# A sixth buffer for the ring of loads in a decoder layer on one core

## The chip, the core and the metric

The kernel runs on one core of a Trainium2 chip. The metric is the time on the device in microseconds (us); less is better. Five engines work side by side, each through its own queue in order: PE (matmul; PEld is its weight load), DVE and ACT (elementwise work), POOL and SP, which issue transfers here. They wait for each other by semaphores. An instruction that waits holds up all that stand behind it on its engine.

## What is computed

One layer of a decoder for 256 tokens of 2048 features, in float32. Cut to what matters here:

```python
mod = silu(c) @ w_ada + b_ada                  # 2048 x 12288: shift, scale, gate, twice
u = x * (1 + scale1) + shift1
proj = u @ w_in                                # 2048 x 9216: GLU input | q | k | v | gate logits
hc = a_lin * sigmoid(a_gate)                   # branch A
hc = silu(layer_norm(causal_depthwise_conv(hc, 31 taps)))
y_conv = hc @ w_conv_out + b_conv_out
y_attn = attention(rope(q), rope(k), v) @ w_attn_out      # branch B: 8 heads, causal
y = (sigmoid(g_A) * y_conv + sigmoid(g_B) * y_attn) @ w_out
x = layer_norm(alpha * x + (1 + gate1) * y)
u = x * (1 + scale2) + shift2
a, val = split(u @ w_up)                       # 2048 x 11264
y = (silu(causal_depthwise_conv(a, 3 taps)) * val) @ w_down
x = layer_norm(alpha * x + (1 + gate2) * y)
```

## The kernel before

All weights are read once from HBM. They come in chunks of 128 rows by 1024 columns (512 KB), 483 of them, called w0, w1, ... here in the order in which they are used. `chunk` (L380) loads a chunk into a `raw` buffer of the pool `st`, casts it on ACT into a high part `wh` (L393), and forms the low part `wl` on DVE by subtracting (L394). `group` (L419) lets PE multiply with it three times (`feat`, L401: L405 high by high, L406 high by the low part of the activations, L407 low by high). The rings hold five `raw` buffers and three each of `wh` and `wl`: the cast of w66 can only start when PE is done with w63.

The matrix w_ada goes past PE: `ada` (L168) loads it in tiles of 512 KB into the same ring of `raw` buffers (the first piece of its columns apart) and sums their rows, weighted by silu(c), on DVE (L207; the first row block on ACT, L205). When a piece of columns is summed over all rows, PE transposes it (L223, eight transposes into two PSUM tiles `pa`), DVE reduces it (L225, two), adds the bias (L234 for the shift, L236 for the scale), and `make_u` (L245) forms four tiles of `u` on ACT (L254), their high parts `uh` (L242), and on DVE their low parts `ul` (L243). A tile of `u` is 128 rows of u, transposed; PE needs tile k for every chunk of w_in that holds rows 128k and up.

The chunks of w_in are taken in an order that lets PE start before all of `u` is there (L655 to L659): w0 to w35 use tiles 0 to 3, w36 to w43 tiles 4 to 7, w44 to w59 tiles 4 to 11, and w60 to w67 are one group with tiles 8 to 15. So w64 is the first that uses tile 12. Chunks w68 to w143 are the rest of w_in, w144 to w159 are w_attn_out, w160 to w175 w_conv_out; then follow w_out, w_up and w_down.

Beside w_in, in the background, run the depthwise conv (L514: products on ACT at L533, sums on DVE at L535 and L531), its layer norm (L538: mean L544, squares L552, variance and square root L557 and L558, reciprocal L560, scaling L566, silu L568, split into `chi` and `clo` at L242 and L243), and the attention of eight heads (L596). In a head the scores `s0` (128 queries by 128 keys) and `s1` (the other 128 queries by 256 keys) get a mask added on DVE (L607 and L608); the left half of the mask for `s1` is zero. Exponentials (L615) follow on ACT. The gates' sigmoids (L490) fall in the same time, and ACT loads a table when it changes between the two. w160, the first chunk of w_conv_out, needs `chi`; the PSUM banks that it writes are freed by four multiplications on DVE (L706).

What stands where in each engine's queue isn't written by hand except at a few places: the framework makes a timeline of its own from the program, its dependencies and its buffers, and orders each engine's instructions by it. So the number of buffers in a ring is one of the things that the order comes from.

Small constants lie in their own tiles: `rows` (L82, six blocks of 128 columns for vectors that PE turns into columns), `rows2` (L113, a seventh), `mask` (L110, 256 columns), `junk` (L218, where L229 writes a copy that nobody reads, since it wants only the row sums), and `bst` (L915, statistics of the last layer norm).

Of the kernel before, what the change touches and what calls it, by code (L numbers as in the profile page):

```python
# [8 lines left out]
F32 = mybir.dt.float32  # L9
F32R = mybir.dt.float32r  # L10
AF = mybir.ActivationFunctionType
OP = mybir.AluOpType
# [21 lines left out]
def layer_kernel(ctx: ExitStack, tc: tile.TileContext, x, c, w_ada, b_ada, w_in, conv_dw_w, conv_dw_b,  # L34
                 conv_ln_g, conv_ln_b, w_conv_out, b_conv_out, w_attn_out, w_out, ln1_g, ln1_b,
                 w_up, ffn_dw_w, ffn_dw_b, w_down, ln2_g, ln2_b, k_ident, k_mask, k_rope, out):
    nc = tc.nc
    x = x[0]
    w_ada, b_ada, w_in, w_conv_out, w_attn_out, w_out, w_up, w_down = (
        t[0] for t in (w_ada, b_ada, w_in, w_conv_out, w_attn_out, w_out, w_up, w_down))  # L40
# [3 lines left out]
    cst = ctx.enter_context(tc.tile_pool(name="cst", bufs=1))  # L44
    big = ctx.enter_context(tc.tile_pool(name="big", bufs=1))
    st = ctx.enter_context(tc.tile_pool(name="st", bufs=5))
    wk = ctx.enter_context(tc.tile_pool(name="wk", bufs=2))
# [5 lines left out]
    def slot(i, shape, dt, name):  # L53
        return big.tile(shape, dt, tag=f"h{i}", name=name)
# [24 lines left out]

# [1 line left out]
    ident = cst.tile([128, 128], F32, name="ident")  # L81
    rows = slot(13, [128, 6, 128], F32, "rows")  # L82
    nc.scalar.dma_start(rows[0:16, 0], c.rearrange("o (r p) -> (o r) p", p=128))
# [19 lines left out]
    ccol, p = columns("ccol", 0, 16)  # L103
# [5 lines left out]
    nc.gpsimd.memset(ones, 1.0)  # L109
    mask = cst.tile([128, 256], F32, name="mask")  # L110
    ropec = cst.tile([128, 256], F32, name="ropec")
    ropes = cst.tile([128, 256], F32, name="ropes")
    rows2 = wk.tile([44, 128], F32, name="rows2", bufs=1)  # L113

    def load_vectors():
        prev = [i for i in traced() if i.engine == mybir.EngineType.SP][-1]

        def put(dst, src):
            nc.gpsimd.dma_start(dst, src)

        r0 = 0
        for ap, n in ((conv_dw_b, 8), (conv_ln_g, 8), (conv_ln_b, 8), (b_conv_out, 16), (ln1_g, 16), (ln1_b, 16),
                      (ffn_dw_b, 44)):
            put(rows[r0:r0 + n, 2], vec(ap))
            r0 += n
        cwr = conv_dw_w.rearrange("k (r p) -> (k r) p", p=128)
        fwr = ffn_dw_w.rearrange("k (r p) -> (k r) p", p=128)
        put(rows[:, 3], cwr[:128])
        put(rows[:120, 4], cwr[128:])
        put(rows[:88, 5], fwr[:88])  # L130
        put(rows2, fwr[88:])
        put(mask, k_mask)
        put(ropec, k_rope[0])
        put(ropes, k_rope[1])

# [1 line left out]
    xT = wide(0, F32, "xT")  # L137
# [19 lines left out]

# [1 line left out]
    mod = cst.tile([128, 96], F32, name="mod")  # L159
# [55 lines left out]
    def to_columns(acc, cols, n, quick=False):  # L215
        w = n * len(cols)
        red = wk.tile([128, 8], F32, tag="red", name="red")
        junk = wk.tile([128, 128], F32, tag="junk", name="junk", bufs=1)  # L218
        for b in range(w // 512):
            p = pst("pa")  # L220
            for i in range(4):
                j = b * 4 + i
                nc.tensor.transpose(p[:, i * 128:(i + 1) * 128], acc[:, j * 128:(j + 1) * 128], ident)  # L223
            if quick:
                nc.vector.tensor_reduce(red[:, b * 4:b * 4 + 4], p.rearrange("p (a b) -> p a b", a=4), AX.X, OP.add)  # L225
            else:
                for i in range(4):
                    j = b * 4 + i
                    nc.scalar.activation(junk, p[:, i * 128:(i + 1) * 128], AF.Copy, accum_out=red[:, j:j + 1])  # L229
        m = n // 128  # L230
# [147 lines left out]

# [1 line left out]
    def chunk(src, width, two=False):  # L380
# [61 lines left out]

# [1 line left out]
    lin = slot(6, [128, 8, 256], F32, "lin")  # L444
# [63 lines left out]

# [1 line left out]
    cacc, chi = [None], []  # L510
# [61 lines left out]

# [1 line left out]
    rps = []  # L574
# [21 lines left out]
    def attention():  # L596
# [4 lines left out]
        def head(h):  # L601
# [4 lines left out]
            p = pp[:, h % 2]  # L606
            nc.vector.tensor_tensor(p[:, 0:128], s0, mask[:, 128:256], OP.add)  # L607
            nc.vector.tensor_tensor(p[:, 128:384], s1, mask, OP.add)  # L608
            mx = wk.tile([128, 6], F32, tag="mx", name="mx")
# [40 lines left out]

# [1 line left out]
    ra0 = 1.0  # L652
# [19 lines left out]
    for i, (g, k0, k1, ra, rb) in enumerate(items):  # L672
# [6 lines left out]
        if i == 12:  # L679
# [11 lines left out]
            p = pst("fw1_ps")  # L691
            nc.tensor.transpose(p[:, :44], rows2, ident[:44, :44])
            fw1 = cst.tile([128, 44], F32, name="fw1")
# [85 lines left out]

# [1 line left out]
    def norm(k, n, center):  # L781
# [38 lines left out]

# [1 line left out]
    NP = 7  # L822
# [49 lines left out]

# [1 line left out]
    lrows = [slot(i, [128, D], F32, n) for i, n in ((14, "l2g"), (15, "l2b"))]  # L874
# [39 lines left out]
    nst = [0, 0]  # L914
    bst = [cst.tile([128, 4 if C2 == 1536 else 5, nc.vector.BN_STATS_DIM], F32, name=f"bst{t}") for t in range(2)]  # L915
    for g, (c0, c1) in enumerate(((0, 1024), (1024, C2), (C2, 2048))):
# [65 lines left out]
```

## Time and profile before

| | us |
|---|---|
| runs | 1475.29, 1480.73, 1479.78 |
| median | 1479.78 |
| span of the profiled execution, first to last instruction | 1477.4 |
| PE busy in it | 1417.7 |
| DVE busy | 1108.8 |
| ACT busy | 796.9 |

The span of the profiled execution lies among the times of the runs, 2.4 us below their median. PE counts as busy from a matmul's start to its end, and matmuls overlap, so short pauses don't show in the busy time. The number behind x in a stretch is the count of matmuls that started in it, and PEclk is the granted clock as a share of 2.4 GHz.

### The profile page before, as it was taken

Reading aid. Unit: us, or ns where it says so; the run is one execution under the profiler, and the core shown is the slowest. Engines: PE = TensorE matmul, PEld = TensorE weight load, DVE = VectorE, ACT = ScalarE, POOL = GpSimd, SP = SyncE. Lnnn points to the kernel's source line nnn. Section 1 sums busy time; section 2 is a strip of 40 time slices with the busy share of each in tenths; the row PEclk is TensorE's granted clock in tenths of the full one; section 3 lists DMA queues with packets and bytes.
Section 4 is the critical chain, followed back from the end, with each engine's and each line's share of the span. In section 5 each row is a group of like instructions: output and inputs, shape, how many; then the busy total and the mean of one; then the engine's idle time right before and its main releaser. Section 6 shows DMA issues by size and latency. Waiting matters only on the chain.

```text
span 1477.4 us, 26835 instructions
## 1 busy us (share of the span) xinstructions
PE 1417.7 (96%) x10691; PEld 1364.2 (92%) x10691; DVE 1108.8 (75%) x1398; ACT 796.9 (54%) x1250; POOL 27.7 (2%) x57
## 2 busy tenths in 40 slices
PE   4899999999999989998999999999999999999996
PEld 4889999989999989997999999999999998888886
DVE  6788888998989879896877767988765545446456
ACT  3546436669987655345545576555444444343342
POOL 2000000210000000000000000000000000000000
PEclk9999999999999999999999999999999999999998
DMA  9999899886567657987799977778776676655662
GB/s 310 328 302 334 299 339 310 256 280 209 175 194 222 210 173 254 310 297 226 242 307 315 323 248 218 240 246 254 238 217 183 180 224 215 193 172 173 189 202 100
DMA packets 154990, 358.53 MB, mean 243 GB/s; under 512 B 12172, under 2 KB 26466, under 8 KB 154608
## 3 DMA queue, kind: packets, MB, share of 16 engines
q1 hardware_dynamic: 152704, 352.37, 74.0%
q0 software_dynamic: 1872, 4.33, 0.9%
q8 instruction: 83, 1.36, 0.4%
q14 instruction: 43, 0.35, 0.1%
q10 hardware_dynamic: 288, 0.12, 0.0%
HBM read 353.10 MB, written 2.10 MB: 240 GB/s over the span
## 4 chain that ended last, share of the span: by engine, by line
PE 75%; DMA 13%; DVE 8%; issue 2%; ACT 2%; SPq 0%; DVEq 0%; ACTq 0%
DMA araw<-in_w_ada_dram 9%; PE acc0a L405 5%; PE acc0a L407 5%; PE acc0a L406 5%; PE acc1a L405 5%; PE acc1a L407 5%; PE acc1a L406 5%; PE acc2a L406 3%; PE acc2a L407 3%; PE acc2a L405 3%; PE acc3a L405 3%; PE acc3a L406 3%; PE acc3a L407 3%; DVE wl L394 3%; DVE acc L207 2%
## 5 line engine op out<-in xcount | busy, mean ns | idle before, releaser
L393 ACT CAST wh<-wraw 128x1024 fp32r<-128x1024 f32 (+1 forms) x483 | 496.7, 1030 | 559.5 <-PE acc3a L416 132.7
L394 DVE TENSOR_TENSOR wl<-wraw,wh 128x1024 fp32r<-128x1024 f32 (+1 forms) x483 | 577.1, 1198 | 252.1 <-ACT wh L393 248.1
L207 DVE SCALAR_TENSOR_TENSOR acc<-araw,ccol,acc 128x1024 f32<-128x1024 f32 (+1 forms) x182 | 225.4, 1238 | 84.3 <-DMA araw<-in_w_ada_dram 82.6
L405 PE MATMUL acc0a<-u2h,wh 128*128 128x256 f32 x352 | 99.3, 282 | 4.8 <-ACT u2h L325 4.8
L407 PE MATMUL acc0a<-u2h,wl 128*128 128x256 f32 x352 | 100.3, 285 | 3.1 <-DVE wl L394 3.1
L405 PE MATMUL acc1a<-u2h,wh 128*128 128x256 f32 x352 | 99.4, 283 | 0.0
L406 PE MATMUL acc0a<-u2l,wh 128*128 128x256 f32 x352 | 99.4, 282 | 0.0
L406 PE MATMUL acc1a<-u2l,wh 128*128 128x256 f32 x352 | 99.2, 282 | 0.0
L407 PE MATMUL acc1a<-u2h,wl 128*128 128x256 f32 x352 | 99.2, 282 | 0.0
L533 ACT ACTIVATE pr<-hc,cw 128x256 f32<-128x256 f32 x200 | 88.8, 500 | 11.7 <-DVE cacc L535 11.3
L405 PE MATMUL acc0a<-uh,wh 128*128 128x256 f32 x256 | 74.9, 292 | 7.1 <-ACT uh L242 7.1
L407 PE MATMUL acc0a<-uh,wl 128*128 128x256 f32 x256 | 74.5, 291 | 3.2 <-DVE wl L394 3.2
L406 PE MATMUL acc0a<-ul,wh 128*128 128x256 f32 x256 | 73.4, 287 | 1.6 <-DVE ul L243 1.6
L405 PE MATMUL acc2a<-uh,wh 128*128 128x256 f32 x256 | 73.1, 286 | 0.5 <-ACT gb L487 0.5
L406 PE MATMUL acc2a<-ul,wh 128*128 128x256 f32 x256 | 73.4, 287 | 0.0
L405 PE MATMUL acc1a<-uh,wh 128*128 128x256 f32 x256 | 73.3, 286 | 0.0
L407 PE MATMUL acc1a<-uh,wl 128*128 128x256 f32 x256 | 73.2, 286 | 0.0
L407 PE MATMUL acc2a<-uh,wl 128*128 128x256 f32 x256 | 73.2, 286 | 0.0
L406 PE MATMUL acc1a<-ul,wh 128*128 128x256 f32 x256 | 73.2, 286 | 0.0
L405 PE MATMUL acc3a<-uh,wh 128*128 128x256 f32 x256 | 73.2, 286 | 0.0
L407 PE MATMUL acc3a<-uh,wl 128*128 128x256 f32 x256 | 73.0, 285 | 0.0
L406 PE MATMUL acc3a<-ul,wh 128*128 128x256 f32 x256 | 72.9, 285 | 0.0
(438 smaller groups left out, 4349.8 us busy)
## 6 DMA issues: line engine op xcount, KB each, us to landing
araw<-in_w_ada_dram SPq DMA_DIRECT2D x176, 512.0 KB, 5.1
wraw<-in_w_up_dram SPq DMA_DIRECT2D x176, 512.0 KB, 4.8
wraw<-in_w_in_dram SPq DMA_DIRECT2D x144, 512.0 KB, 4.9
wraw<-in_w_down_dram SPq DMA_DIRECT2D x55, 512.0 KB, 4.5
wraw<-in_w_down_dram SPq DMA_DIRECT2D x44, 384.0 KB, 3.7
wraw<-in_w_out_dram SPq DMA_DIRECT2D x32, 512.0 KB, 5.5
araw<-in_w_ada_dram SPq DMA_DIRECT2D x32, 256.0 KB, 5.7
wraw<-in_w_attn_out_dram SPq DMA_DIRECT2D x16, 512.0 KB, 4.5
```

The source lines that it names most:

```text
L207: op = nc.vector.scalar_tensor_tensor(acc, r, ccol[:, k:k + 1], acc, OP.mult, OP.add)
L393: nc.scalar.copy(wh, raw)
L394: nc.vector.tensor_tensor(wl, raw, wh.bitcast(F32), OP.subtract)
L405: nc.tensor.matmul(o, wh[:, cs], ah, start=first and i % 2 == 0, stop=False, skip_group_check=True)
L406: nc.tensor.matmul(o, wh[:, cs], al, start=False, stop=False, skip_group_check=True)
L407: nc.tensor.matmul(o, wl[:, cs], ah, start=False, stop=last, skip_group_check=True)
L533: nc.scalar.activation(pr[:, k % 2, i], src, AF.Copy, scale=w)
```

## The change

The pool `st` gets `bufs=6`, so the ring of `raw` has six buffers of 4 KB a partition. To make room

- `rows2` becomes a seventh block of `rows`;
- `mask` keeps its right half alone. In a head, DVE adds it to `s0` and to the right half of `s1`; the left half of `s1` is copied by ACT;
- L229 writes its unused copy over its own input in PSUM, and `junk` goes;
- `bst` lies in the memory of `bada` (the bias of w_ada).

```diff
-    st = ctx.enter_context(tc.tile_pool(name="st", bufs=5))
+    st = ctx.enter_context(tc.tile_pool(name="st", bufs=6))
...
-    rows = slot(13, [128, 6, 128], F32, "rows")
+    rows = slot(13, [128, 7, 128], F32, "rows")
...
-    mask = cst.tile([128, 256], F32, name="mask")
+    mask = cst.tile([128, 128], F32, name="mask")
...
-    rows2 = wk.tile([44, 128], F32, name="rows2", bufs=1)
...
-        put(rows2, fwr[88:])
-        put(mask, k_mask)
+        put(rows[:44, 6], fwr[88:])
+        put(mask, k_mask[:, 128:])
...
-        junk = wk.tile([128, 128], F32, tag="junk", name="junk", bufs=1)
...
-                    nc.scalar.activation(junk, p[:, i * 128:(i + 1) * 128], AF.Copy, accum_out=red[:, j:j + 1])
+                    nc.scalar.activation(p[:, i * 128:(i + 1) * 128], p[:, i * 128:(i + 1) * 128], AF.Copy, accum_out=red[:, j:j + 1])
...
-            nc.vector.tensor_tensor(p[:, 0:128], s0, mask[:, 128:256], OP.add)
-            nc.vector.tensor_tensor(p[:, 128:384], s1, mask, OP.add)
+            nc.vector.tensor_tensor(p[:, 0:128], s0, mask, OP.add)
+            nc.scalar.copy(p[:, 128:256], s1[:, 0:128])
+            nc.vector.tensor_tensor(p[:, 256:384], s1[:, 128:256], mask, OP.add)
...
-            nc.tensor.transpose(p[:, :44], rows2, ident[:44, :44])
+            nc.tensor.transpose(p[:, :44], rows[:44, 6], ident[:44, :44])
...
-    bst = [cst.tile([128, 4 if C2 == 1536 else 5, nc.vector.BN_STATS_DIM], F32, name=f"bst{t}") for t in range(2)]
+    bst = [bada[:, t * 30:t * 30 + 30].rearrange("p (a b) -> p a b", a=5) for t in range(2)]
```

SP issues the same loads in the same order. PE, DVE and ACT get their instructions in another order in many places; three of them follow. Line numbers of the changed kernel are one or two lower from the middle of the file on.

PE, where the transposes for tiles 12 to 15 of `u` (`pa`) stand beside the chunks w61 (`wh_2431`), w63 (`wh_2522`) and w64 (`wh_2587`), before:

```order
L223 MATMUL pa_2555<-ident_70,acc_1852 128x128 x4
L223 MATMUL pa_2561<-ident_70,acc_1852 128x128
L405 MATMUL acc0a_2416<-uh1_95,wh_2431 128x256
...
L223 MATMUL pa_2561<-ident_70,acc_1852 128x128 x3
...
L405 MATMUL acc0a_2416<-uh1_95,wh_2522 128x256
...
L405 MATMUL acc0a_2416<-uh1_95,wh_2587 128x256
```

And after, where w63 is `wh_2517` (low part `wl_2518`) and w64 is `wh_2581`:

```order
L221 MATMUL pa_2549<-ident_70,acc_1848 128x128
...
L404 MATMUL acc3a_2414<-ul1_96,wh_2517 128x256
L405 MATMUL acc3a_2414<-uh1_94,wl_2518 128x256
L221 MATMUL pa_2549<-ident_70,acc_1848 128x128 x3
L221 MATMUL pa_2555<-ident_70,acc_1848 128x128 x4
L403 MATMUL acc0a_2411<-uh1_94,wh_2581 128x256
```

Seven of the eight transposes moved from before w63 to the place right ahead of w64's first matmul. ACT at the same place, before (casts of w63, w64, w65, w66 are `wh_2522`, `wh_2587`, `wh_2620`, `wh_2653`):

```order
L393 CAST wh_2522<-wraw_2520 128x1024
L393 CAST wh_2587<-wraw_2585 128x1024
L254 ACTIVATE u_2569<-xT1_92,mod_93 128x256
...
L242 CAST uh1_95<-u_2569 128x256
L242 CAST uh1_95<-u_2573 128x256
L393 CAST wh_2620<-wraw_2618 128x1024
L242 CAST uh1_95<-u_2577 128x256
...
L393 CAST wh_2653<-wraw_2651 128x1024
```

And after (`wh_2517`, `wh_2581`, `wh_2614`, `wh_2647`):

```order
L391 CAST wh_2517<-wraw_2515 128x1024
L391 CAST wh_2581<-wraw_2579 128x1024
L391 CAST wh_2614<-wraw_2612 128x1024
L391 CAST wh_2647<-wraw_2645 128x1024
L252 ACTIVATE u_2563<-xT1_91,mod_92 128x256
...
L240 CAST uh1_94<-u_2563 128x256
```

The casts of w65 and w66 moved ahead of the four `u` and the four `uh`. On DVE the reductions moved with them: the row there is now L207, two L225, L394 of w66, L234, L207, L236, where it was L225, L207, L225, L234, L394 of w63, L207, L236.

ACT in the attention, where the sigmoids of `ga` (L490 before, L488 after) meet the exponentials (L615 and L614), before:

```order
L490 ACT_TABLE_LOAD
L490 ACTIVATE ga_1064<-ga_1064 128x512 x2
L533 ACTIVATE pr<-hc,cw_1551 128x256 x2
L490 ACTIVATE ga_1064<-ga_1064 128x512
L242 CAST ohi<-po 128x256
L625 COPY pp<-tp 128x384
L490 ACTIVATE ga_1064<-ga_1064 128x512
L393 CAST wh<-wraw 128x1024
```

And after:

```order
L488 ACT_TABLE_LOAD
L488 ACTIVATE ga_1061<-ga_1061 128x512
...
L614 ACT_TABLE_LOAD
L614 ACTIVATE pp,mx<-pp,mx 128x128
L614 ACTIVATE pp,mx<-pp,mx 128x256
L488 ACT_TABLE_LOAD
L488 ACTIVATE ga_1061<-ga_1061 128x512
L531 ACTIVATE pr<-hc,cw_1551 128x256 x2
L391 CAST wh<-wraw 128x1024
L606 COPY pp<-s_4479 128x128
```

An exponential now stands between the sigmoids, and behind them others follow; L606 is the new copy. In all ACT has 15 table loads after and 11 before.

ACT at the layer norm behind the conv, before (the last cast here is w162, the first ones w158 and w159):

```order
L393 CAST wh<-wraw 128x1024 x2
L544 ACTIVATE pr<-pm 128x256
L393 CAST wh<-wraw 128x1024
L552 ACTIVATE sq<-cacc 128x1024 x2
L393 CAST wh<-wraw 128x1024
L555 ACT_TABLE_LOAD
...
L393 CAST wh<-wraw 128x1024
L568 ACT_TABLE_LOAD
L568 ACTIVATE cacc<-cacc,vecs 128x256 x2
L242 CAST chi<-cacc 128x256
```

And after (the first ones end with w156, the last cast is w161):

```order
L391 CAST wh<-wraw 128x1024 x4
L542 ACTIVATE pr<-pm 128x256
L391 CAST wh<-wraw 128x1024
L550 ACTIVATE sq<-cacc 128x1024 x2
L391 CAST wh<-wraw 128x1024
...
L391 CAST wh<-wraw 128x1024 x2
L566 ACT_TABLE_LOAD
L566 ACTIVATE cacc<-cacc,vecs 128x256 x2
L391 CAST wh<-wraw 128x1024
L240 CAST chi<-cacc 128x256
```

The mean and the squares moved forward by three chunks, and one cast now stands between the first silu and the first `chi`. On DVE the first `clo` moved ahead of the last two of the four L706.

## Rows read from the trace of the kernel before

**Rows 1.** Busy us, share of the span, instructions, by engine.
```profile
PE 1417.7 (96%) x10691; PEld 1364.2 (92%) x10691; DVE 1108.8 (75%) x1398; ACT 796.9 (54%) x1250; POOL 27.7 (2%) x57
```
**Rows 2.** Stages: stretch, its us, PE busy (matmuls), PEclk, DMA share, GB/s.
```profile
40.00:200.00 160.00, 149.81 (x1168) 0.98 0.93 318
...
520.00:560.00 40.00, 34.73 (x256) 0.91 0.57 179
...
640.00:720.00 80.00, 72.10 (x517) 0.96 0.75 240
720.00:840.00 120.00, 116.93 (x967) 1.00 0.92 309
840.00:1440.00 600.00, 600.00 (x4302) 1.00 0.69 214
```
**Rows 3.** Waits of PE: line, for whom, us in total, times, longest.
```profile
PE acc0a L405 <- ACT uh L242: 7.1, 3, 4.6
PE acc0a L407 <- DVE wl L394: 6.3, 9, 2.2
PE acc0a L405 <- ACT chi L242: 5.3, 1, 5.3
...
PE acc0a L405 <- ACT wh L393: 2.0, 1, 2.0
```
**Rows 4.** Waits of SP's queue of loads, the longest.
```profile
SPq L388 <- DVE wl L394: 347.0, 181, 4.3
```
**Rows 5.** Stretches of 10 us, PE, columns as in rows 2.
```profile
50.00:60.00 10.00, 5.38 (x29) 0.70 1.03 358
60.00:70.00 10.00, 10.00 (x82) 0.95 0.99 349
...
90.00:100.00 10.00, 7.78 (x53) 1.00 0.95 322
...
530.00:540.00 10.00, 6.74 (x35) 0.66 0.35 111
```
**Rows 6.** DVE in order of time: start us, us, line, operation, tiles.
```profile
225.89 0.69 DVE L225 TENSOR_REDUCE red<-pa 128x4 f32<-128x512 f32 x1
226.49 0.16 DVE L234 TENSOR_TENSOR mod<-red,bada 128x4 f32<-128x4 f32 x1
226.56 1.22 DVE L394 TENSOR_TENSOR wl<-wraw,wh 128x1024 fp32r<-128x1024 f32 x1
227.70 1.28 DVE L207 SCALAR_TENSOR_TENSOR acc<-araw,ccol,acc 128x1024 f32<-128x1024 f32 x1
228.89 0.16 DVE L236 SCALAR_TENSOR_TENSOR mod<-red,bada 128x4 f32<-128x4 f32 x1
```
**Rows 7.** ACT in order of time, the same place.
```profile
229.97 2.08 ACT L254 ACTIVATE u<-xT,mod 128x256 f32<-128x256 f32 x4
231.96 0.70 ACT L242 CAST uh<-u 128x256 fp32r<-128x256 f32 x2
```
**Rows 8.** PE in order of time, the same place.
```profile
232.40 0.38 PE L405 MATMUL acc0a<-uh,wh 128*128 128x256 f32 x1
```
**Rows 9.** Stretches of 40 us, ACT busy (instructions), then as in rows 2.
```profile
360.00:400.00 40.00, 38.38 (x83) 1.00 0.59 174
400.00:440.00 40.00, 35.41 (x68) 1.00 0.63 183
440.00:480.00 40.00, 31.10 (x55) 1.00 0.72 224
```
**Rows 10.** Groups on ACT: count, busy us, mean ns of one, idle before.
```profile
L229 ACT ACTIVATE junk<-pa 128x128 f32<-128x128 f32 x48 | 13.3, 276 | 4.1 <-PE pa L223 3.1
...
L490 ACT ACT_TABLE_LOAD x2 | 2.6, 1283 | 0.0
```

## Prediction

> **What bounds the kernel now.** I read the busy times first [rows 1]: PE is busy for 96% of the span, DVE for 75%, ACT for 54%, so only time that PE loses can be won. Next came the stages [rows 2]. In 840 to 1440 us PE is busy for 600.00 of 600.00 while the DMA engines are at 0.69; there an earlier load is worth nothing. PE loses time in four places: 40 to 200 us and 720 to 840 us, where the DMA engines stand at 0.93 and 0.92, and 520 to 560 and 640 to 720 us, where they are at 0.57 and 0.75 and something else must be late. The waits of PE name them [rows 3]: 7.1 us for `uh` (4.6 of it at once), 5.3 us for `chi`, and for the weights themselves 6.3 us (`wl`) and 2.0 us (`wh`). The queue of loads (SP) waits far longer for its buffers, 347.0 us on one line alone [rows 4], but mostly in stretches in which PE has all it needs.
>
> A long wait costs PE more than its length. The stretch 50 to 60 us holds the 4.6 us wait and carried 29 matmuls at a granted clock of 0.70; the next carried 82 at 0.95 [rows 5]. The 53 missing ones are worth 53 x 10/82 = 6.5 us, so about 2 us were lost to the half level (1.2 GHz) after the wait. 530 to 540 us, after the `chi` wait, shows the same: 35 matmuls at 0.66. The 2.2 us wait in 90 to 100 us left the clock at 1.00.
>
> **The sixth buffer.** SP's instructions keep their order, and every load is of the same bytes; a load may only start one buffer, 512 KB, earlier. What that can win is bounded by the waits for weights, 6.3 + 2.0 = 8.3 us [rows 3], and from below by nothing. In 40 to 200 us the loads ran at 318 GB/s with the engines at 0.93 [rows 2], and the best ten microseconds shown went at 358 GB/s [rows 5]: some slack, but the stretch with the 4.6 us wait is that best one, so this wait is not for want of a buffer. I take some fifth of the bound, **-1.5 us**.
>
> That stretch is also where a rule speaks against the change. The Trainium skill, "DMA: Bandwidth & Descriptors", section Specifications, gives about 358 GB/s as the limit of HBM for one core; the trace agrees with its 358. By the rule no depth of ring makes the loads of 50 to 60 us come sooner, and this term would be near 0 in place of -1.5.
>
> **The moved instructions.** The ring is one of the things from which the scheduler's own timeline is made, and with six buffers it writes the three compute engines' queues in another order. That counts for more than the buffer.
>
> *The fourth quarter of u (w64).* Chunk w64 is the first that multiplies by rows 12 to 15 of `u`. In the trace before, the chain from the second `TENSOR_REDUCE` at 225.89 us to the first `uh` cast at 231.96 (end 232.31 at 0.35 each) runs beside PE's work on earlier chunks, and PE's first matmul of w64 starts at 232.40 with no idle time ahead of it [rows 6 to 8]: it just fits. In the new order seven of the eight transposes that begin this chain stand on PE behind all matmuls of w63 and right ahead of w64's first. ACT now casts w65 and w66 ahead of the four `u`; w66 takes the `wh` buffer that w63 frees. So nothing of the chain can pass PE's end of w63, and PE has nothing else in its queue. From start to start [rows 6, 7]: two reduces 2 x 0.60, L394 of w66 1.14, L234 0.07, L207 1.19, L236 0.16, four `u` 1.99, one `uh` 0.35: 1.20 + 1.14 + 0.07 + 1.19 + 0.16 + 1.99 + 0.35 = **+6.1 us**. The first reduce may run beside the last transposes (down to 5.6); the L207 that now stands ahead of it may hold it for its 1.28 (up to 7.4). Since this wait is longer than the 4.6 us one, I add the same loss to the half level, **+2 us** (0 to 2.6).
>
> *Attention and conv.* The mask's zero half is replaced by a copy on ACT, 8 of 128x128 out of PSUM; the nearest row is L229's 0.276 us [rows 10], 2.2 us in all, while DVE's add loses half its columns and so can only save. The order also alternates `exp` and `sigmoid` more often: ACT has 15 table loads where it had 11, and 4 x 1.283 = 5.1 us [rows 10]. That is 7.3 us on ACT, in the stage where ACT is fullest: 38.38 and 35.41 of 40 us [rows 9], 6.2 us of slack in 80. The next 40 us have 8.9. Bounds are 0 (all hidden by the slack and by the three `wh` buffers) and 7.3. Since the four extra loads stand within 45 rows of ACT's queue, near the fullest rows, I take **+6.5 us** as PE's loss.
>
> *The layer norm behind the conv (`chi`).* Its chain has moved earlier by about three chunks: on ACT the mean stands after cast w156 where it stood after w159, and the square root of the variance after w158 where it stood after w161. Gone with it would be the 5.3 us wait and what the half level cost: in 530 to 540 us 82 - 35 = 47 matmuls are missing, 47 x 10/82 = 5.7 us, of which 3.3 are idle [rows 5], so 2.4. But on ACT cast w161 now stands between the first silu and `chi`, and on DVE two of the four L706 that free the PSUM banks stand behind the first `clo`, so a wait of some 3 to 4 us can be left in small pieces. Bounds -7.7 and 0; I take **-3.5 us**.
>
> *The rest at nothing.* The in-place output of L229, the statistics in `bada`'s place and the seventh row of `rows` change addresses only: the same engines do the same number of instructions, and `bada` is read for the last time long before the down projection. If the last were wrong, the end of the kernel would show it in whole waits.
>
> **Sum** against the profiled execution: -1.5 + 6.1 + 2 + 6.5 - 3.5 = **+9.6 us** on a span of 1477.4, so 1487.0. The median of the three runs lies 2.4 us above that span, so I forecast 1479.8 + 9.6 = **1489 us**, 0.65% slower.
>
> **Rivals.**
> - *The ring pays* (the faster side). If the loads come so early that the last w_ada row of that quarter is summed well ahead, the scheduler's order still lets seven transposes stand last, so the chain stays; but the price could shrink to the 5.6, with the clock held (0), all 8.3 us of weight waits gone, ACT's additions hidden (0) and `chi` free (-7.7): 5.6 - 8.3 - 7.7 = -10.4, about 1469; half of the last two gains gives -2.4. It decides at the point where the gains pass 8 us. For it speaks the long wait of SP [rows 4]; against it that PE is full where SP waits most [rows 2]. The Trainium skill, "Perfetto Trace Analysis", section Optimization Strategy, says that the same gap repeated on the engine that should be full can mean too few buffers. By that rule the kernel would gain those 8.3 us at most, but here the repeated gap is on SP and not on PE.
> - *The gains and losses cancel.* The exposed chain costs 6.1 + 2, ACT's additions are mostly hidden (+2), the `chi` wait goes whole (-7.7) and the ring brings -2: +0.4, 1480. For it speaks that ACT has slack on both sides of its fullest rows [rows 9], against it the order of the first `clo`.
> - *The buffer does nothing.* The loads are held by their rate, the ring's term is 0 and only the order is left, with ACT's whole addition and no gain at `chi`: 6.1 + 2 + 7.3 = +15.4, 1495. For it speaks 358 GB/s as the best row [rows 5]; against it 0.93 and 318 GB/s over 160 us [rows 2].
>
> **How the numbers follow.** I give 0.50 to the forecast (+5 to +13), 0.15 to the buffer doing nothing (above +13), 0.25 to cancelling (-5 to +5) and 0.10 to the ring paying (below -5). The top of the range is the chain, the clock and ACT at their upper bounds with nothing gained, 7.4 + 2.6 + 7.3 = +17.3, 1497; the bottom takes in the cancelling case, -5, 1475. That leaves out about 0.15. A difference of 0.5%, 7.4 us, is about what a measurement of this kernel can tell from no change. The forecast's +9.6 lies 2 us beyond that bound: of its 0.50 I put 0.42 beyond it, since the largest term, the chain, is the surest. With the 0.15 that makes 0.57 for slower. Of the 0.10 below -5, 0.08 are faster by more than 7.4, and 0.35 remain between.
>
> **What would show it.** Right: a new idle time of PE of about 6 us near 220 to 230 us, ended by ACT's `uh`, with a stretch of granted clock near 0.7 behind it; ACT with 15 table loads, and PE no longer full between 380 and 440 us; the 5.3 us `chi` wait gone or in pieces, and the clock at 1.00 there; PE's waits for `wl` below 6.3 us. The first 200 us should be at most 3 us shorter. Wrong: no idle time of PE at w64 (the chain was hidden by something that I don't see), or the load-bound stretches shorter by more than 8 us, or a new wait at the end of the kernel.

## The result and the profile after

The changed kernel takes 1490.44 us (median of four runs, 1489.21 to 1492.41), the kernel before, beside it, 1480.26. The ratio is 1.0063, 95% interval 1.0037 to 1.0088: slower, by 0.4% to 0.9%. The forecast was 1489, with 1475 to 1497 as its range. The total is right; most of the terms under it are not, as the experiments show. (One of the twelve runs of after_old_w64 below took 1982.8 us at a granted clock of 0.657 and is left out of its median and ratio.)

The busy times of the profiled execution (columns as in [rows 1]); its span is 1488.0 us, 10.6 us longer than before, while PE's busy time is only 3.7 us longer:

```profile
PE 1421.4 (96%) x10691; PEld 1365.6 (92%) x10691; DVE 1106.1 (74%) x1398; ACT 801.8 (54%) x1262; POOL 27.7 (2%) x57
```

The stages of [rows 2], after (stretch, its us, busy us and count of PE, PEld, DVE, ACT, POOL, then PEclk, DMA share, GB/s):

```profile
40.00:200.00 160.00, 154.87 (x1233) 151.80 (x1232) 139.22 (x149) 82.67 (x116) 0.00 (x0) 0.99 0.96 337
...
520.00:560.00 40.00, 35.91 (x259) 34.64 (x258) 26.26 (x31) 19.44 (x28) 0.00 (x0) 0.91 0.62 193
...
640.00:720.00 80.00, 70.37 (x490) 66.32 (x489) 59.58 (x85) 35.73 (x78) 0.00 (x0) 0.94 0.72 234
720.00:840.00 120.00, 120.00 (x1000) 119.79 (x1000) 95.64 (x107) 64.97 (x96) 1.45 (x2) 1.00 0.93 310
840.00:1440.00 600.00, 598.49 (x4295) 563.71 (x4294) 380.68 (x476) 296.81 (x422) 2.53 (x4) 1.00 0.69 216
```

In 40 to 200 us PE started 1233 matmuls where it had started 1168, at 337 GB/s in place of 318. That is a large gain, and it is the first sign that the small term for the buffer was wrong. The waits of PE after (line, for whom, us, times, longest), to be read against [rows 3]:

```profile
PE acc0a L403 <- ACT uh L240: 11.9, 4, 5.9
PE acc0a L405 <- DVE wl L392: 7.9, 8, 1.6
...
PE acc0a L403 <- ACT wh L391: 2.1, 2, 1.8
...
PE acc0a L403 <- ACT chi L240: 0.5, 1, 0.5
```

The wait for `uh` grew by 4.8 us, that for `chi` is gone in name, and that for the weights did not shrink. The new wait for `uh` is at w64, in order of time (start us, us, engine, line, operation, tiles):

```profile
223.60 1.28 DVE L206 SCALAR_TENSOR_TENSOR acc<-araw,ccol,acc 128x1024 f32<-128x1024 f32 x1
224.79 1.28 DVE L223 TENSOR_REDUCE red<-pa 128x4 f32<-128x512 f32 x2
225.99 1.22 DVE L392 TENSOR_TENSOR wl<-wraw,wh 128x1024 fp32r<-128x1024 f32 x1
...
227.20 1.28 DVE L206 SCALAR_TENSOR_TENSOR acc<-araw,ccol,acc 128x1024 f32<-128x1024 f32 x1
228.39 0.15 DVE L234 SCALAR_TENSOR_TENSOR mod<-red,bada 128x4 f32<-128x4 f32 x1
...
228.58 2.08 ACT L252 ACTIVATE u<-xT,mod 128x256 f32<-128x256 f32 x4 [3.28 <-DVE mod L234]
230.56 1.31 ACT L240 CAST uh<-u 128x256 fp32r<-128x256 f32 x4
...
224.18 0.93 PE L221 MATMUL pa<-ident,acc 128*128 128x128 f32 x7
231.00 0.58 PE L403 MATMUL acc0a<-uh,wh 128*128 128x256 f32 x1 [5.90 <-ACT uh L240]
```

It is the chain of the prediction link by link: seven transposes, two reductions, the `wl` of w66, L206, L234, four `u`, `uh`, then PE. Four stretches of 10 us around the two places of [rows 5 to 8] show the clock:

```profile
220.00:230.00 10.00, 5.10 (x44) 4.87 (x42) 9.23 (x11) 3.51 (x5) 0.00 (x0) 0.92 0.98 341
230.00:240.00 10.00, 9.00 (x59) 9.00 (x60) 4.08 (x7) 3.96 (x8) 0.00 (x0) 0.74 0.60 196
530.00:540.00 10.00, 5.98 (x44) 5.17 (x42) 9.95 (x13) 6.89 (x14) 0.00 (x0) 0.95 0.47 133
540.00:550.00 10.00, 9.93 (x61) 9.88 (x62) 8.02 (x12) 4.64 (x7) 0.00 (x0) 0.71 0.67 205
```

To see where time went I numbered in each trace the 10,344 matmuls that read `wh` or `wl`, and subtracted the start of the n-th in the trace of before. The column is the time of that matmul in before; a negative number is a lead. The columns stand, within one chunk, at w7, w49, w61, w65, w74, w95, w139, w167, w211, w243 and w279. (In the expectations below, the names of chunks given for PE's loss, and those of matmuls moved on PE, come from dividing the matmuls evenly over the chunks and are up to nine too high: w67, w72, w81, w99 and w148 there stand for w61, w65, w74, w95 and w139 here.)

```
                     55    191    227    238    261    324    466    559    716    812    920
after              -1.0   -7.5   -8.3    0.4    1.2    5.2    6.8    6.5   12.9    9.0   10.8
five_old_order     -1.7   -1.6   -1.6   -1.8   -1.8   -1.7   -1.7   -1.2   -1.1   -1.0   -0.1
six_old_order      -1.2   -7.1   -7.1   -7.2   -7.2   -7.2   -7.2   -7.2  -10.4  -14.3  -14.8
six_old_order_act  -2.8  -10.8  -10.8  -10.9  -10.9  -10.9   -1.6   -2.4   -3.7   -7.5   -8.0
six_more_tables    -1.7   -7.5   -7.5   -7.6   -7.6   -7.6   -4.8   -4.9   -8.1  -12.0  -12.5
six_new_w64        -1.3   -7.3   -8.2    0.4    0.4    0.4    0.4    0.1   -3.2   -7.1   -7.6
six_new_mid        -2.1   -6.6   -6.6   -6.7   -6.7   -3.3   -0.2   -1.9   -2.2   -6.1   -6.6
after_old_w64      -3.0   -8.4   -8.4   -8.5   -3.3    0.5    1.6   -0.3    5.5    1.6    3.7
after_old_w81      -2.2   -7.4   -7.4   -7.6   -7.6   -4.2   -2.3   -2.8    1.6   -0.2    3.1
after_dve_mask     -2.3   -8.6   -9.5   -0.9   -0.8    3.1    3.9    1.7    9.3    5.4    8.8
six_free_order     -2.0   -7.7   -8.6   -0.1    1.4    5.1    5.1    3.2    3.1    2.2    6.6
six_chi_early      -1.9   -7.3   -7.3   -7.4   -7.4   -7.4   -7.4  -13.2  -15.5  -19.4  -19.9
six_chi_early2     -2.3  -10.6  -10.6  -10.7  -10.7  -10.7  -10.7  -17.2  -19.8  -23.7  -24.2
```

The first row holds the whole result: 8.3 us gained by 227 us, 8.7 lost at w64, 4.8 lost by 324, 1.6 in the attention (324 to 466), 0.3 gained around `chi`, 6.4 lost by 716, 3.9 gained by 812, 1.8 lost at the end: +10.8. These are differences of single executions, and up to 1.6 of the 8.3 us may not be the change's: five_old_order, with the order and the five buffers of before, has that lead too. Its wait for `uh` at 50 us was 3.5 us, that of the execution of before 4.6.

### The profile page after: what moved, and what is told of

Read it like the earlier page. It is cut to its first block, busy times and chain, and to the rows that moved or that the text cites. A ratio compares the mean times of both kernels' runs of the same rounds, so it can differ in the third digit from the quotient of the medians.

```text
span 1488.0 us, 26850 instructions
## 1 busy us (share of the span) xinstructions
PE 1421.4 (96%) x10691; PEld 1365.6 (92%) x10691; DVE 1106.1 (74%) x1398; ACT 801.8 (54%) x1262; POOL 27.7 (2%) x57
## 4 chain that ended last, share of the span: by engine, by line
PE 73%; DMA 11%; DVE 8%; ACT 6%; issue 3%; DVEq 0%; SPq 0%; ACTq 0%
DMA araw<-in_w_ada_dram 9%; PE acc0a L405 5%; PE acc0a L403 5%; PE acc0a L404 5%; PE acc1a L404 5%; PE acc1a L403 4%; PE acc1a L405 4%; DVE wl L392 3%; PE acc2a L403 3%; PE acc2a L404 3%; PE acc2a L405 3%; PE acc3a L403 3%; PE acc3a L404 3%; PE acc3a L405 3%; DVE acc L206 2%
## 5 line engine op out<-in xcount | busy, mean ns | idle before, releaser
L206 DVE SCALAR_TENSOR_TENSOR acc<-araw,ccol,acc 128x1024 f32<-128x1024 f32 (+1 forms) x182 | 225.3, 1238 | 101.2 <-DMA araw<-in_w_ada_dram 100.3
L404 PE MATMUL acc0a<-u2l,wh 128*128 128x256 f32 x352 | 99.2, 282 | 0.0
L404 PE MATMUL acc1a<-u2l,wh 128*128 128x256 f32 x352 | 99.1, 281 | 0.0
L404 PE MATMUL acc0a<-ul,wh 128*128 128x256 f32 x256 | 73.7, 288 | 0.6 <-DVE ul L241 0.6
L404 PE MATMUL acc1a<-ul,wh 128*128 128x256 f32 x256 | 73.5, 287 | 0.0
L404 PE MATMUL acc2a<-ul,wh 128*128 128x256 f32 x256 | 73.0, 285 | 0.0
L404 PE MATMUL acc3a<-ul,wh 128*128 128x256 f32 x256 | 73.0, 285 | 0.0
```

Source lines behind the costliest of these rows:

```text
L206: op = nc.vector.scalar_tensor_tensor(acc, r, ccol[:, k:k + 1], acc, OP.mult, OP.add)
L404: nc.tensor.matmul(o, wh[:, cs], al, start=False, stop=False, skip_group_check=True)
```

## Experiments

The change is two things at once: a buffer, and another order of the instructions. To part them, a function `pin` writes out an engine's whole order. It reads a table (`ORDER`, the positions of the instructions of PE, DVE and ACT in the program) and chains each to the one before it, in issue order only, in place of the loop at the end of the kernel. "Old order" is the order of the kernel before, "new order" that of the changed kernel.

```diff
-        for n, i in enumerate(seq):
-            if w and n >= w and i.name in lazy:
-                order(seq[n - w], i)
...
+        for a, b in zip(want, want[1:]):
+            order(seq[a], seq[b])
```

The new order with five buffers wasn't tried: by my reading, which no run shows, an instruction would wait in it for a load whose buffer is freed only behind it. Where DVE carries the mask, the edit is this, and DVE's count stays that of before:

```diff
-            nc.vector.tensor_tensor(p[:, 0:128], s0, mask, OP.add)
-            nc.scalar.copy(p[:, 128:256], s1[:, 0:128])
-            nc.vector.tensor_tensor(p[:, 256:384], s1[:, 128:256], mask, OP.add)
+            ends = [t.rearrange("p (a b) -> p a b", b=128)[:, 0:3:2] for t in (p, s01[:, 0:384])]
+            nc.vector.tensor_tensor(*ends, mask[:, None, :].to_broadcast([128, 2, 128]), OP.add)
+            nc.vector.tensor_copy(p[:, 128:256], s1[:, 0:128])
```

Measured, each against the kernel before on the same chip. The chip is not the same for all rows (five_old_order and six_old_order ran on two), but the kernel before took 1480.26 to 1481.43 us on each:

| kernel | median us | ratio to before | 95% interval |
|---|---|---|---|
| after | 1490.44 | 1.0063 | 1.0037 to 1.0088 |
| five_old_order | 1480.94 | 0.9995 | 0.9985 to 1.0005 |
| six_old_order | 1464.03 | 0.9891 | 0.9866 to 0.9915 |
| six_new_w64 | 1471.88 | 0.9939 | 0.9927 to 0.9952 |
| after_old_w64 | 1485.40 | 1.0035 | 1.0018 to 1.0053 |
| after_old_w81 | 1478.89 | 0.9990 | 0.9976 to 1.0005 |
| six_old_order_act | 1473.77 | 0.9948 | 0.9931 to 0.9965 |
| after_dve_mask | 1488.56 | 1.0070 | 1.0043 to 1.0097 |
| six_free_order | 1486.19 | 1.0040 | 1.0024 to 1.0056 |
| six_more_tables | 1466.57 | 0.9906 | 0.9892 to 0.9921 |
| six_new_mid | 1469.22 | 0.9916 | 0.9902 to 0.9930 |
| six_chi_early | 1461.68 | 0.9866 | 0.9852 to 0.9879 |
| six_chi_early2 | 1458.36 | 0.9846 | 0.9830 to 0.9863 |

### The buffer alone

```diff
-    st = ctx.enter_context(tc.tile_pool(name="st", bufs=5))
+    st = ctx.enter_context(tc.tile_pool(name="st", bufs=6))
```

> Six buffers, with PE, DVE and ACT held to the order of the kernel before; the mask costs ACT nothing (one DVE instruction adds it to both 128-column ends, one DVE instruction copies the middle, so DVE's count stays). Only the buffer is left of the change. In the trace of the changed kernel PE reaches w63 8.3 us earlier than before. Theory A, the buffer made that lead: 1472 (1469 to 1475), PE at w63 7 to 9 us ahead of before and no idle time of PE over 2 us at w64. Theory B, the new order made the lead and the buffer alone gives what was forecast for it, -1.5: 1478 to 1480, PE at w63 at most 2 us ahead. Theory C, the lead is the buffer's, but PE then waits at w64 in the old order too, since the sums of w_ada come no earlier: 1476 to 1480 with an idle time of 3 to 6 us there.

> six_old_order with five buffers in place of six, all else the same (mask on DVE, statistics in bada's place, order of the kernel before). If the 16.6 us that six_old_order gained are the buffer's: 1479 to 1482, the time of the kernel before, with PE's waits for wl and wh back between 90 and 190 us and between 750 and 810 us. If the rewritten mask or the fixed order made them: 1464 to 1470.

With five buffers, the pinned order and the rewritten mask the time is that of before (0.9995). With six it is 1464.0, and that pair differs in the number of buffers alone: the buffer is worth some 16 us (15.4 by the ratios, 16.9 by the medians). That is theory A in its lead at w64, and more in the total than theory A gave. The stages with five:

```profile
40.00:200.00 160.00, 150.98 (x1178) 146.84 (x1177) 133.97 (x145) 80.09 (x112) 0.00 (x0) 0.98 0.94 323
640.00:720.00 80.00, 71.68 (x524) 68.22 (x525) 60.17 (x83) 42.25 (x90) 0.00 (x0) 0.98 0.75 243
720.00:840.00 120.00, 116.76 (x959) 115.14 (x958) 91.64 (x96) 59.54 (x88) 1.45 (x2) 1.00 0.92 307
```

and with six:

```profile
40.00:50.00 10.00, 10.00 (x86) 10.00 (x85) 8.15 (x9) 6.58 (x11) 0.00 (x0) 1.00 1.03 362
...
40.00:200.00 160.00, 154.21 (x1229) 151.14 (x1228) 138.63 (x149) 83.06 (x115) 0.00 (x0) 0.99 0.96 335
640.00:720.00 80.00, 73.42 (x562) 71.04 (x562) 63.23 (x89) 41.10 (x71) 0.00 (x0) 0.98 0.77 258
720.00:840.00 120.00, 120.00 (x1004) 120.00 (x1003) 91.21 (x90) 67.96 (x110) 2.43 (x4) 1.00 0.94 326
```

In all three stages the loads run 4% to 6% faster (335 over 323, 258 over 243, 326 over 307 GB/s) and PE starts 51, 38 and 45 more matmuls. The lead comes in the same three places, 5.5, 3.3 and 5.3 us (five_old_order against six_old_order, up to 227, from 559 to 716, and on to 920). The waits of PE in six_old_order:

```profile
PE acc0a L403 <- ACT uh L240: 5.8, 2, 3.5
PE acc0a L403 <- ACT chi L240: 5.2, 1, 5.2
...
PE acc0a L405 <- DVE wl L392: 1.5, 2, 1.0
PE acc0a L403 <- ACT wh L391: 1.1, 1, 1.1
```

Against [rows 3] those for `wl` and `wh` fell by 4.8 and 0.9 us, that for `uh` by 1.3, and that for `ul` (L406 before, L404 here) from 1.6 to 0.6. All that the view lists for PE behind its first chunk fell from 28.6 to 19.9 us, 8.7 of the 14.8. The other 6 show in no wait of the view: they lie in pauses between matmuls too short to be listed and in stretches at the half level, and only the starts of the matmuls have them.

### The place at w64

Three kernels swap the two orders in that place alone; the rows are those shown with the change. six_new_w64 puts the new order into six_old_order, after_old_w64 the old one into the changed kernel, after_old_w81 goes on with the old one for ten more chunks.

> six_old_order with the changed kernel's order in one place only, around w64 (the place that after_old_w64 undid). If the place costs what the changed kernel's trace shows (6.2 us idle, then the half level, 8.7 us between w67 and w72) and nothing gives it back: 1464.0 + 8.7 = 1472.7 (1471.5 to 1474). If it costs only the 5 us that undoing it returned, because the loads and DVE catch up while PE stands: 1468 to 1470.

> The changed kernel, with the order of before on PE, DVE and ACT in one place only, around w64 (ACT: casts w65 to w67 and the four tiles of u; DVE: w62 to w71; PE: the matmuls of w62 to w66 and the eight transposes). If the exposed chain costs what the trace shows, 6.2 us idle and some 2.5 us at the half level behind it: 1482 (1480 to 1484), 8 to 9 us less than the changed kernel, no idle time of PE over 1 us at w64. Rival: the sums of w_ada are late there in any order, and PE waits at w64 as long: 1488 to 1491.

> after_old_w64 with the order of before kept on to w81 (DVE, ACT and PE), the rest in the changed kernel's order. after_old_w64 won 8.5 us by w72 and lost 5 of them from w77 to w81 to waits for wl. If these come from DVE's new order behind w71: they go, and the lead at w81 is -8 against before; the waits at w85 to w95 (4 us) stay: 1482 to 1483. If they come from the loads, which PE overtakes when it no longer stands at w64: they come a little later instead, 1485 to 1486.

The place costs 7.8 us when put in (1471.9 against 1464.0, ratios 0.9939 and 0.9891), and its trace has the same wait of 5.90 us for `uh` and no other from 215 to 262 us:

```profile
231.18 0.58 PE L403 MATMUL acc0a<-uh,wh 128*128 128x256 f32 x1 [5.90 <-ACT uh L240]
```

Taken out of the changed kernel it gave 1485.4, between the two expectations, and its interval overlaps that of the changed kernel: in the trace the wait is gone and the lead at 238 us is -8.5, but at 261 it is -3.3. PE's waits in after_old_w64 from 240 to 262 us:

```profile
PE acc0a L405 <- DVE wl L392: 3.6, 2, 2.3
```

With the old order kept to w81 the lead at 261 us is -7.6 and that wait is gone (1478.9, with an interval clear of the changed kernel's): so it came from the new order behind w64, which was late with `wl` as soon as PE no longer stood still ahead of it, and not from the loads. after_old_w81 beat its expectation by 3 us in the median; its profiled execution, with a span of 1483.7, is one of its longer ones and loses some 3 us more after 920 us, so I don't read its last columns.

### The mask and the tables on ACT

> As six_old_order, but with the mask as in the change: a copy of 128 columns on ACT in each of eight heads, the rest of ACT in the order of before. If a copy costs no more than its own 0.276 us, eight of them cost 0 to 2.2 us against six_old_order. If the hand-over counts (scores on PE, copy on ACT behind casts and products that stand ahead of it, then the reduction on DVE, then the exponential on ACT again), each head comes 1 us or more later, and PE waits for the heads' transposes: 8 us or more against six_old_order, with new idle times of PE between 360 and 450 us.

> The changed kernel in its own order, with the eight copies of the mask taken from ACT (one DVE instruction adds the mask to both ends, one copies the middle). PE loses 6.4 us between w72 and w148 against before. If that is the copies' own time: 2 us less, 1488.5. If it is the hand-over in the heads: 5 to 6 us less, 1485. If it is the order alone (15 table loads, sigmoids between exponentials): 1490, no change, and the losses stay where they are.

> The changed kernel with the mask on DVE (one instruction for both ends, one copy) and the order left to the framework. ACT has 11 table loads, as before the change, and no copies; the seven transposes still stand right ahead of w64. So this takes away what the prediction charged ACT in the attention, copies and table loads together. If the prediction's +6.5 for them is right: 1490.4 - 6.5 = 1484, and PE loses nothing more between w99 and w148. If the trace's reading is right, that only 1.6 of the 6.4 us that PE loses between w72 and w148 lie in the attention and the rest in waits for wl ahead of it: 1488 to 1489. The 6.2 us at w64 stay in both.

> six_old_order with two of the first gate's four sigmoids moved behind the next two heads' exponentials on ACT, so that ACT loads four tables more (15 in place of 11) in its fullest stretch, and nothing else. If ACT's slack hides them: 1464 (0 to +1.5). If they lie on the path, as the prediction counted them: 4 x 1.283 = +5.1, 1469, with idle times of PE ahead of the heads' transposes between 370 and 400 us.

six_old_order_act: +9.7 us over six_old_order for eight copies of 0.25 us each, lost between 324 and 466 us (9.3 in the trace). The hand-over is what costs. DVE and ACT there in order of time:

```profile
357.36 0.28 DVE L605 TENSOR_TENSOR pp<-s,mask 128x128 f32<-128x128 f32 x1
362.25 0.29 DVE L607 TENSOR_TENSOR pp<-s,mask 128x128 f32<-128x128 f32 x1 [4.61 <-ACT pp L606]
...
359.17 1.15 ACT L488 ACTIVATE ga<-ga 128x512 f32<-128x512 f32 x2
360.22 0.90 ACT L531 ACTIVATE pr<-hc,cw 128x256 f32<-128x256 f32 x2
361.02 1.03 ACT L391 CAST wh<-wraw 128x1024 fp32r<-128x1024 f32 x1
361.95 0.26 ACT L606 COPY pp<-s 128x128 f32<-128x128 f32 x1
```

and PE's waits from 340 to 420 us:

```profile
PE tp L623 <- DVE pp L607: 3.2, 1, 3.2
PE po L630 <- ACT pp L624: 1.6, 1, 1.6
PE pa L221 <- DVE pp L607: 0.7, 1, 0.7
```

The copy stands behind sigmoids, products and a cast; DVE's second addition, which is ordered behind it, stands idle for 4.61 us with everything queued after it, and PE's transpose of the head comes 3.2 us late. These waits are 5.5 of the 9.3 us. In the changed kernel's own order the copies have better places: taking them away there (after_dve_mask) makes no difference that the times show; in its trace 324 to 466 us cost 0.8 in place of 1.6 us, a difference of two single executions. Left to the framework without the copies (six_free_order) that stretch costs nothing, ACT has 11 table loads again, and the time is 1486.2. The 4 us that this kernel gains are not clear of the noise (the intervals overlap), and nearly all of them lie elsewhere (716 us: +3.1 in place of +12.9, some of it lost again later). So it was the copies that brought the four table loads. The order at w64, whose wait is in this trace too (5.9 us), came without them; that the sixth buffer brought it, and not one of the other moves that make room, no kernel here separates. Four table loads more in the old order (six_more_tables) cost 2.8 us in the trace, half of the 5.1 that I counted; the medians differ by 2.5, with intervals that overlap. PE's waits there, 360 to 410 us:

```profile
PE tp L623 <- ACT pp L618: 1.7, 1, 1.7
...
```

### The middle of the kernel in the new order

> six_old_order with the changed kernel's order from w81 to w170 only (end of w_in, attention without the copies on ACT, conv, its layer norm). In after_dve_mask PE lost 4.5 us against before from w81 to w148 and won 3 at chi. If that holds with no idle time at w64 ahead of it: +1 to +4, 1465 to 1468. If that order lives from the idle time at w64, in which DVE and the loads catch up (after_old_w64 lost 8.8 us from w72 to w94, where the changed kernel lost 4.8): +5 to +9, 1469 to 1473, with PE waiting for wl between w76 and w95.

The edit is w81 to w170 on DVE and ACT, with PE's work that goes with it. By the trace it is 8.2 us behind six_old_order by 571 us: 0.5 ahead of the edited place, 3.4 by 324, with 2.2 us of listed waits for `wl`, 3.1 in the attention, 1.2 net around `chi` and what follows. This execution is the longest of its five runs, 3.3 us above their median. The median is 5.2 us above six_old_order, with intervals that just overlap (0.9915 and 0.9902). That is the second expectation's size, but not its picture alone: the listed waits for `wl` are no longer than the changed kernel's there (3.3), and the attention adds as much.

### The layer norm behind the conv

In six_old_order the chain to `chi` waited for PE twice, ACT 1.12 us for the sum `pm` and DVE 1.32 us for `pv`: both stood behind matmuls that were not urgent. The edit moves them, and the conv's last products, forward; on ACT:

```diff
-L531 ACTIVATE pr<-hc,cw_1551 128x256 x2
-L391 CAST wh<-wraw 128x1024 x2
-L531 ACTIVATE pr<-hc,cw_1551 128x256 x2
+L531 ACTIVATE pr<-hc,cw_1551 128x256 x4
...
+L566 ACTIVATE cacc<-cacc,vecs 128x256
+L240 CAST chi<-cacc 128x256
+L566 ACTIVATE cacc<-cacc,vecs 128x256
+L240 CAST chi<-cacc 128x256
+L391 CAST wh<-wraw 128x1024
```

> six_old_order with the layer norm behind the conv moved by hand: the last two pairs of conv products ahead of the casts of w155 and w156, mean, squares and square root one to two chunks earlier on ACT and DVE, the sums over features (pm, pv) 33 and some 60 matmuls earlier on PE, the L705 that free the banks between the scalings, and three sums of w_ada behind the split. In six_old_order PE waits 5.4 us for chi and then has a stretch at the half level. If nothing else is late there: 5.4 + some 2.5 less, 1456 (1455 to 1458). If the wait only changes its name (clo, or wl of w161 to w164, since DVE is given more to do in that place): 1460 to 1464.

> six_chi_early with two of the three sums of w_ada that it put behind the split given back earlier places (into pauses of DVE behind the clo of the third and the last group). In six_chi_early PE lost 2.4 us again to a wait for wl at w176 to w184, where DVE stood 2.7 us for a tile of w_ada that was loaded late because its buffer had been held. If that is why: 1459 to 1460, 2 us less than six_chi_early. If the loads are at their rate there: no change, 1461 to 1462.

six_chi_early: the wait for `chi` and the stretch at the half level are gone, and 7.5 us are gained by w163 (547 us); 2.4 are then lost to `wl`, as DVE stands idle for a late tile of w_ada:

```profile
537.60 1.28 DVE L206 SCALAR_TENSOR_TENSOR acc<-araw,ccol,acc 128x1024 f32<-128x1024 f32 x1 [2.70 <-DMA araw<-in_w_ada_dram]
538.81 3.49 DVE L392 TENSOR_TENSOR wl<-wraw,wh 128x1024 fp32r<-128x1024 f32 x3
```

In the median it gained 2.4 us where 8 were hoped for, and its interval overlaps that of six_old_order. six_chi_early2 lets two of DVE's sums go ahead of a `wl`, so that their buffers come free sooner:

```diff
+L206 SCALAR_TENSOR_TENSOR acc<-araw,ccol,acc 128x1024
 L392 TENSOR_TENSOR wl<-wraw,wh 128x1024
 L241 TENSOR_TENSOR clo<-cacc,chi 128x512
 L206 SCALAR_TENSOR_TENSOR acc<-araw,ccol,acc 128x1024
-L392 TENSOR_TENSOR wl<-wraw,wh 128x1024
-L206 SCALAR_TENSOR_TENSOR acc<-araw,ccol,acc 128x1024
-L392 TENSOR_TENSOR wl<-wraw,wh 128x1024
+L392 TENSOR_TENSOR wl<-wraw,wh 128x1024 x2
```

It takes 1458.4 us, the shortest time of all (ratio 0.9846, 0.9830 to 0.9863); the interval overlaps that of six_chi_early, so the second step alone isn't shown to gain; both together are clear of six_old_order (0.9866 to 0.9915). The 20 us around `chi` in six_old_order:

```profile
520.00:540.00 20.00, 14.84 (x102) 14.51 (x101) 14.35 (x20) 12.09 (x19) 0.00 (x0) 0.83 0.41 127
```

and in six_chi_early2, with 58 matmuls more and the clock at full:

```profile
520.00:540.00 20.00, 19.26 (x160) 19.06 (x159) 15.08 (x17) 9.60 (x13) 0.00 (x0) 1.00 0.77 241
```

## Why the prediction was right and where it was wrong

*The sixth buffer, -1.5 (0 to -8.3): wrong, by ten times.* It is worth some 16 us (ratio 0.9891). Two steps failed. The bound was taken from PE's waits for `wl` and `wh` [rows 3]. These fell by 5.7 us; but where loads set the pace they also delay the sums of w_ada, and through them `uh` and `ul`: 3 us came from waits under such other names, and 6 from pauses that no wait lists and from the half level. A bound that would have held lies in the count of matmuls, if the full stretch is read rightly. The 82 of the prediction started at a clock of 0.95; at full clock it is 86. But the matmuls of `v` (w16 to w19) have 512 columns and take 227 ns each where the others take 120 (medians, from start to start), and a stretch with some of them is full with 53. In the kernel before (columns as in [rows 2]):

```profile
80.00:90.00 10.00, 10.00 (x53) 1.00 0.90 293
...
540.00:550.00 10.00, 10.00 (x86) 1.00 0.52 156
```

With the 48 matmuls of 512 columns counted twice, the 1168 of [rows 2] are 16 x 86 - 1168 - 48 = 160 short, 160 x 10/86 = 18.6 us in this stage alone. It is a bound and no estimate: with six buffers 5.5 us of it came back. And the stretch of 358 GB/s was read as the loads' limit. It was not: six_old_order moved 362 GB/s in the ten microseconds ahead of it, where the kernel before has 305, and the kernel before itself moved 360 at 210 to 220 us. The forecast's own test, that the first 200 us should be at most 3 us shorter, failed: they are 7.5 us shorter. With the 3.9 us of 716 to 812 us the load-bound stretches are shorter by more than the 8 us that the prediction named as a sign of being wrong, and the waits for `wl`, 7.9 us, did not fall below 6.3.

The rival of which the prediction gave the page, "Perfetto Trace Analysis" of the Trainium skill, section Optimization Strategy (the same gap, repeated, can mean too few buffers), had the sign of this term right though its 8.3 us were half of it. The 358 GB/s that the Trainium skill gives as the limit for a core ("DMA: Bandwidth & Descriptors", section Specifications) did not bind: the traces have rows above it, as that page's section Bandwidth allows for a core whose neighbour is idle, which I passed over. Whether the neighbour was idle here no run shows.

*w64, +6.1 and +2: right.* 5.90 us of wait, 8.7 us of loss in the trace, 7.8 alone. The chain ran as written and the granted clock fell to 0.74 in the stretch behind it.

*Attention, +6.5: wrong in size.* The cost was put at nearly all of ACT's added time, and it is 1.6 us in the changed kernel's own trace; from 380 to 440 us, where the forecast had PE no longer full, it is busy for 59.64 of 60 us. By the traces four table loads more cost 2.8 of their 5.1 us in the old order and at most 0.8 in the new one without the copies; the copies cost nothing that the times show where the scheduler found them a place, and 9.7 us where the rest of the order was held.

*`chi`, -3.5: wrong.* The wait lost its name and came back in pieces (the freed banks, 2.3 us, `wl`, 1.2, and 0.5 of `chi`), and the clock, forecast at 1.00, fell all the same (0.71 in 540 to 550 us); 0.3 us were gained. That a wait of 3 to 4 us "can be left in small pieces" was written down and then half of the gain was counted anyway. PE's waits from 520 to 560 us after:

```profile
PE acc3a L403 <- DVE gb L705: 1.3, 1, 1.3
PE acc0a L405 <- DVE wl L392: 1.2, 1, 1.2
PE acc2a L403 <- DVE gb L705: 1.0, 1, 1.0
...
```

*At nothing: right.* No listed wait behind 1440 us; from 920 us on the loss keeps within 0.2 us. five_old_order, which has all the address changes, equals the kernel before.

*Not in the sum: the order elsewhere.* 4.8 us by 324 us, 6.4 from 559 to 716, 1.8 after 812, 13 us in all, 7.9 of it in listed waits for `wl` that before does not have in these places (3.3, 3.2 and 1.4). I looked at the order in three places and took the rest to be alike. Only of the first was a part tested on its own (six_new_mid, 3.4 us by 324 us); the others are read from the trace. Over the whole kernel the order that came with the change, copies included, took 26 us (1490.4 against 1464.0) where the buffer gave 16. The wait for `u2h`, 4.8 us between 560 and 720 us, which the prediction's list of waits leaves out, is the same before and after.

So the sum came out by luck, by two large errors that cancel: the buffer was put too low by 10.7 us as it shows in this trace (8.3 + 3.9 - 1.5, which counts in the 1.6 that five_old_order has too) and `w64` by 0.6, the attention too high by 4.9, `chi` too favourable by 3.2, and 13.0 were missing: -10.7 + 0.6 - 4.9 + 3.2 + 13.0 = +1.2, which is 10.8 - 9.6.

## What to carry to other kernels

Where an order is derived from the program, a changed buffer count is two changes; hold the order fixed to see what the buffer is worth, and then mend the order. Bound what faster loads can win by the matmuls that a stage is short of, counted by their columns, not by the listed waits for weights. A small operation handed to another engine can cost what stands ahead of it in that queue: here 9.7 us for eight copies of 0.25.

## What the hardware showed that was not expected

The loads' best ten microseconds are no ceiling: 358 GB/s before [rows 5], 362 in six_old_order, and in six_chi_early2, a kernel with the same loads, 383 and 396 at 50 to 70 us; over 40 us six_chi_early moved 366 (91 to 131 us). And a wait of PE of the same length left the clock in three different ways. At 50 us each of the three kernels below waits for `uh` for 3.5 us; the granted clock in the stretch was 0.66 in five_old_order, 0.83 in six_old_order and 1.00 in six_chi_early2, which is 3.4, 1.7 and 0 us of the full clock given away, part of it during the wait itself (2.4 GHz is full, 1.2 the lower level); 32, 43 and 57 matmuls are counted in it. five_old_order:

```profile
50.00:60.00 10.00, 6.48 (x32) 6.27 (x31) 6.66 (x10) 5.03 (x8) 0.00 (x0) 0.66 0.98 351
```

six_old_order:

```profile
50.00:60.00 10.00, 6.48 (x43) 6.25 (x42) 7.36 (x11) 5.48 (x9) 0.00 (x0) 0.83 0.96 328
```

six_chi_early2:

```profile
50.00:60.00 10.00, 6.83 (x57) 6.83 (x58) 8.50 (x12) 5.51 (x9) 0.00 (x0) 1.00 1.04 383
60.00:70.00 10.00, 10.00 (x86) 10.00 (x85) 10.00 (x13) 3.23 (x4) 0.00 (x0) 1.00 1.03 396
```

So up to 3 us of a single execution's lead at 50 to 70 us are not the order's (compare six_old_order_act and six_chi_early2 at 191 us with six_old_order, which has the same order up to there), for a reason that no trace here shows, and a price of the half level from one profiled execution is good to about that much.
